# Paged decode attention inside a hybrid step: the five score stages of a half batch issued as one run in front of the value products

## The chip, the cores and the metric

The kernel runs on one core of one Trainium2 chip. The metric is the device time of one execution in microseconds (us). The kernel before took 1226.16 us (median of three executions, 1226.01 to 1227.58).

## The reference

One layer of a decoder serves 512 prompt tokens and 8 sequences of 4 new tokens each with shared weights. Cut to what the change touches, the latent attention of the new tokens over their paged past:

```python
past_c = cache_kv_latent[l][page_table].reshape(Bs, past_len, KV_LORA)   # 8 x 4096 x 256
past_r = cache_k_rope[l][page_table].reshape(Bs, past_len, QK_ROPE)      # 8 x 4096 x 64
s = (einsum('bqhr,bsr->bhqs', ql, c_kv) + einsum('bqhd,bsd->bhqs', qr, k_rope)) * scale
p = softmax(where(k_pos <= qp, s, -inf))
o = einsum('bhqs,bsr->bqhr', p, c_kv)
```

Around it stand two gated feed-forward blocks, a gated linear recurrence, the prompt's own attention and the projections, all in fp32.

## The kernel before

The large products take each fp32 operand as a high and a low part and sum three products (lines 225 to 262). While the decode attention runs (0.71 to 0.93 ms of the span) two generators are interleaved by the loop at line 1645: `decode()` (line 1557), and `phase_a()` (line 728), which finishes the second half of the output projection and runs the first 8 column tiles of the second feed-forward block for the prompt. The matmuls of `phase_a` are line 248: 128 rows by 128 columns of weights, 256 or, from 738 us on, 512 moving columns.

Decode works on 16 halves, two per sequence; a half is 2048 past keys in two blocks. For each half:

- `gather` (line 1477) and `gather_r` (line 1486): POOL issues indirect DMAs that bring the latent rows into one of seven slots (`ma`, `dx0`, `dx1`, `q0`, `ha`, `hb`, `mb`) and the rotary rows into `rraw`.
- `turn(st)` (line 1493): two 32x32 block transposes on VectorE (DVE, line 1498) write one stage of turned keys into a buffer `kh`. Stage 0 is the rotary part, stages 1 to 4 are 64 latent columns each. There are `KHB` = 4 buffers.
- `score(st)` (line 1501): eight products of 64 rows by 32 columns (line 1510; the profile counts each fp32 product as two matmuls, so 16), one in each of the eight 64x32 tiles of the array. After the last stage ScalarE (ACT) copies the odd column groups to `odd` (line 1518), and DVE adds them and takes the maximum (line 1519), called "top" below.
- `peak` (line 1521): a small matmul `pm` (line 1523) turns the maxima; DVE reduces (1525) and scales (1528); ACT takes the exponential (1529); DVE transposes to `pt` (1531); six ACT copies and two DVE copies spread it into `pbuf` (1537).
- `value(mate, c)` (line 1539): eight products of 128 rows by 32 columns for each block (line 1546; 16 matmuls in the profile).

Below, S run means score products of line 1510 that follow each other, V run the 32 value matmuls of a half, S(k) and V(k) those of half k (0 to 15), top(k) and pm(k) likewise.

The step loop at lines 1577 to 1605 places these. In iteration `n` it scores half n-2, takes the peak of half n-3 at step 1 and its values at step 4, and turns one stage per step. `RUNS` says that stages 0, 1, 2 are scored at step 2 and stages 3, 4 at step 4, in front of the values. The build then orders each engine's instructions by its own list scheduler, so a run as written can be cut where it places other ready work in between. A shared helper `tmp` (line 161) hands out scratch tiles by tag, two buffers each; `ssq` and `sq1` are also used by the sums of squares of lines 677, 717 and 267, which end before half 1 is scored.

Of the kernel before, what the change touches and what calls it, by code (L numbers as in the profile page):

```python
# [9 lines left out]
F32 = mybir.dt.float32  # L10
# [5 lines left out]
ALU = mybir.AluOpType  # L16
AX = mybir.AxisListType

P = 128
# [22 lines left out]
ROWS = 8  # L42
# [17 lines left out]
NW = 2  # L60
PRE, BODY = 22, 95
JS = ((8, 9), (0, 1), (2, 3), (4, 5), (6, 7))
KHB = 4
PEAK = 1
RUNS = {2: (0, 1, 2), 4: (3, 4)}
LEVELS = (32, 16, 8, 4, 2, 1)
CH = 64

# [39 lines left out]
def hybrid_step_kernel(  # L108
# [5 lines left out]
    nc = tc.nc  # L114
# [12 lines left out]
    def mk(shape, dt, tag, bufs=1, pool=None):  # L127
        return (pool or cur[-1]).tile(shape, dt, name=tag, tag=tag, bufs=bufs)
# [32 lines left out]
    def tmp(tag, n, bufs=2, pool=sb):  # L161
        return mk([P, HM], F32, tag, bufs, pool=pool)[:, :n]
# [70 lines left out]
    def gemm(wt, act_):  # L233
        wh, wl, kt = wt
        acc = ps("acc", "acc")
        n = act_[0].shape[-1]
        mm3(acc[:, :n], [((wh[:, k], wl[:, k]), (act_[0][:, k], act_[1][:, k])) for k in range(kt)])
        return acc[:, :n]
# [309 lines left out]
    with scope("ffn0") as pool:  # L548
# [4 lines left out]
        l, r = [u[:, lo4] for u in ux], [u[:, hi4] for u in ux]  # L553
# [56 lines left out]
        if True:  # L610
            if True:
                sst.close()
                st = stg.enter_context(tc.tile_pool(name="st", bufs=1, side="right", reuse_waits="tile"))
# [198 lines left out]
    with scope("mix") as mx_:  # L812
# [291 lines left out]
        with scope("at2"):  # L1104
# [6 lines left out]
            with scope("kv"):  # L1111
# [43 lines left out]
                for g in range(2):  # L1155
                    w = weight([w_qr[2 * g + i] for i in range(2)], KQ)
                    a = [gemm(w, Q[x]) for x in BOTH]
# [262 lines left out]
    with scope("dec"):  # L1420
# [48 lines left out]
        class Half:  # L1469
# [23 lines left out]
            def turn(self, st):  # L1493
                kh = mk([P, 2, ROWS, 2, 32], F32, "kh", KHB)
                j = JS[st][0]
# [5 lines left out]
            def score(self, st):  # L1501
                q = qbd[self.b % 2]
                if st == 0:
                    self.s = [ps("s", own=True) for _ in range(2)]
                for jj, j in enumerate(JS[st]):
                    for g in range(2):
                        c = (2 * jj + g) * 32
                        for r in range(2):
                            rs = slice(r * 64, r * 64 + 64)
                            nc.tensor.matmul(self.s[r][c : c + 32, : 2 * P], q[rs, j], self.kh[st][rs, g, :, jj], start=st == 0, stop=st == len(JS) - 1, skip_group_check=True)  # L1510
                if st == 1 and self.i and self.b + 1 < NB:
                    qsplit(self.b + 1)
                if st < len(JS) - 1:
                    return
                odd = mk([64, 2, 2 * P], F32, "odd")
                self.mx = mk([P, 1], F32, "mxh", 2)
                for r in range(2):
                    nc.scalar.copy(odd[:, r], self.s[r][64:, : 2 * P])
                    self.top = nc.vector.tensor_tensor_reduce(self.e[r * 64 : r * 64 + 64], self.s[r][:64, : 2 * P], odd[:, r], 1.0, -3.0e38, ALU.add, ALU.max, self.mx[r * 64 : r * 64 + 64])

            def peak(self):
                pm = ps("pm", "pm")[:, :P]
                nc.tensor.matmul(pm, self.mx.broadcast_to([P, P]), ident, start=True, stop=True, skip_group_check=True)
                m = m3[:, self.i, self.bs]
                nc.vector.tensor_reduce(m, pm.rearrange("p (g q) -> p q g", q=16), axis=AX.X, op=ALU.max)
                mq = mk([P, 16], F32, "mq", 2)
                mb = mk([P, 1], F32, "mbd", 2)
                nc.vector.scalar_tensor_tensor(mq, m, -SCALE, selL, op0=ALU.mult, op1=ALU.mult, accum_out=mb)
                nc.scalar.activation(self.e, self.e, AF.Exp, scale=SCALE, bias=mb, accum_out=Lc[:, self.i, 0, self.b : self.b + 1])
                pt = mk([P, ROWS, 32], F32, "pt", 2)  # L1530
                nc.vector.transpose(pt.rearrange("p a k -> p (a k)"), self.e)
                for r in range(2):
                    for g in range(2):
                        for h_ in range(2):
                            src = pt[(2 * r + g) * 32 : (2 * r + g) * 32 + 32, :, h_ * 16 : h_ * 16 + 16]
                            to = self.p[(2 * r + h_) * 32 : (2 * r + h_) * 32 + 32, g, :, self.i * 16 : self.i * 16 + 16]
                            (nc.scalar.copy if g + h_ else nc.vector.tensor_copy)(to, src)
# [19 lines left out]
        def decode():  # L1557
            H = [Half(n) for n in range(NH2)]
            blocks = [h_ for h_ in H for _ in range(2)]
            ups = [(h_, st) for h_ in H for st in range(len(JS))]  # L1560

            def gather(n=1):
                for h_ in blocks[:n]:
                    h_.gather()
                del blocks[:n]

            def turn(top):
                if ups:
                    h_, st = ups.pop(0)
                    if h_.n + st == 0:  # L1570
                        top = pin[0]
                    with tc.issue_after(top.ins) if top is not None else nullcontext():
                        h_.turn(st)
                    if st == 0 and h_.n + 1 < NH2:
                        H[h_.n + 1].gather_r()

            for n in range(NH2 + 4):

                def at(k):
                    return H[n - k] if 0 <= n - k < NH2 else None  # L1580

                for st in range(len(JS)):
                    if at(2):
                        for k in RUNS.get(st, ()):
                            at(2).score(k)
                    if n < 2 and st == 0:
                        if n == 0:
                            H[0].gather_r()
                        gather(2)
                        if n:  # L1590
                            nc.gpsimd.memset(pbuf, 0.0)
                    if n == 2 and st == 3:
                        gather(3)
                    if st == PEAK and at(3):
                        at(3).peak()
                    if st == 1 and at(4) and at(4).i:
                        at(4).gathered()
                    if st == len(JS) - 1 and at(3):
                        for c in range(2):
                            at(3).value(at(4), c)  # L1600
                            gather()
                    if n > 1 or n == 1 and st >= 1:
                        if n != 2 or st >= 2:
                            turn(at(2).top if at(2) and st == len(JS) - 1 else None)
                    yield

        def decode_end():
            uvf = mk([P, 2, NH, P], F32, "kh", KHB)
            for j in range(2):
# [130 lines left out]
    with scope("ffn1") as pool:  # L1740
# [96 lines left out]
        st = stg.enter_context(tc.tile_pool(name="st2", bufs=1, side="right", reuse_waits="tile"))  # L1837
# [113 lines left out]
```

## Time and profile before

| | before |
|---|---|
| median of three executions | 1226.16 us |
| the profiled execution | 1225.88 us |
| its span, first to last instruction | 1224.0 us |
| TensorE matmul (PE) busy | 1197.8 us, 98% |
| VectorE (DVE) busy | 986.6 us, 81% |
| ScalarE (ACT) busy | 693.6 us, 57% |
| line 1510, score matmuls | 1280, 47.2 us busy |

Busy time of an engine counts the time in which at least one of its instructions runs; matmuls overlap each other, so a matmul of 0.38 us does not cost 0.38 us. What a matmul costs is read from the distance between starts in the timeline. The profiled execution spent 1.9 us outside its span.

### The profile page before, as it was taken

Reading aid. Unit: us, or ns where it says so; the run is one execution under the profiler, and the core shown is the slowest. Engines: PE = TensorE matmul, PEld = TensorE weight load, DVE = VectorE, ACT = ScalarE, POOL = GpSimd, SP = SyncE. Lnnn points to the kernel's source line nnn. Section 1 sums busy time; section 2 is a strip of 40 time slices with the busy share of each in tenths; the row PEclk is TensorE's granted clock in tenths of the full one; section 3 lists DMA queues with packets and bytes.
Section 4 is the critical chain, followed back from the end, with each engine's and each line's share of the span. In section 5 each row is a group of like instructions: output and inputs, shape, how many; then the busy total and the mean of one; then the engine's idle time right before and its main releaser. Section 6 shows DMA issues by size and latency. Waiting matters only on the chain.

```text
span 1224.0 us, 26742 instructions
## 1 busy us (share of the span) xinstructions
PE 1197.8 (98%) x10924; PEld 1092.4 (89%) x10924; DVE 986.6 (81%) x2008; ACT 693.6 (57%) x1447; POOL 97.7 (8%) x112
## 2 busy tenths in 40 slices
PE   8999999999999999999999999999999999999997
PEld 7999999999999989998998876666667999999996
DVE  7997887878678788886877789888985789778665
ACT  7765554454476654554758765455444465554373
POOL 0000000000000000000000123332321111000000
PEclk9999999999999999999999999999999999999999
DMA  6233333323254313333242486679876858533451
GB/s 242 70 121 104 104 101 94 101 80 105 83 186 142 116 56 104 90 92 108 95 141 86 163 343 209 231 266 356 277 258 163 262 211 286 163 107 118 103 149 74
DMA packets 78427, 188.43 MB, mean 154 GB/s; under 512 B 14032, under 2 KB 35568, under 8 KB 73824
## 3 DMA queue, kind: packets, MB, share of 16 engines
q1 hardware_dynamic: 58128, 115.50, 28.8%
q0 software_dynamic: 15440, 65.67, 16.5%
q10 hardware_dynamic: 4736, 5.55, 1.3%
q8 instruction: 85, 1.39, 0.5%
q14 instruction: 38, 0.31, 0.1%
HBM read 170.53 MB, written 16.16 MB: 153 GB/s over the span
## 4 chain that ended last, share of the span: by engine, by line
PE 81%; issue 6%; DVE 5%; ACT 3%; DMA 3%; POOL 1%; DVEq 0%; SPq 0%; ACTq 0%; POOLq 0%
PE acc L248 18%; PE dn L230 12%; PE Y L449 11%; PE acc L230 8%; PE Z L449 7%; PE X L449 7%; PE acc L1853 3%; PE acc L628 3%; PE s L1510 3%; PE o L1546 2%; DVE kh L1498 1%; DMA ma<-w_g 1%; PE pa L976 1%; DMA mb<-w_u 1%; PE s L1226 1%
## 5 line engine op out<-in xcount | busy, mean ns | idle before, releaser
L248 PE MATMUL acc<-uh,wh 128*128 128x272 f32 (+2 forms) x496 | 160.9, 324 | 0.0
L248 PE MATMUL acc<-ul,wh 128*128 128x272 f32 (+2 forms) x496 | 156.3, 315 | 1.0 <-DVE ul L196 1.0
L248 PE MATMUL acc<-uh,wl 128*128 128x272 f32 (+2 forms) x496 | 155.7, 314 | 0.5 <-issue 0.5
L230 PE MATMUL dn<-hh,dh 128*128 128x272 f32 x384 | 111.3, 290 | 0.1
L230 PE MATMUL dn<-hh,dl 128*128 128x272 f32 x384 | 110.7, 288 | 0.0
L230 PE MATMUL dn<-hl,dh 128*128 128x272 f32 x384 | 110.5, 288 | 0.0
L222 DVE TENSOR_TENSOR wl<-wraw,wh 128x1024 fp32r<-128x1024 f32 (+2 forms) x78 | 83.6, 1074 | 31.7 <-ACT wh L221 31.1
L248 PEld LDWEIGHTS acc<-uh,wh 128*128 128x128 f32 x496 | 93.4, 188 | 17.1 <-issue 12.7
L221 ACT CAST wh<-wraw 128x1024 fp32r<-128x1024 f32 (+2 forms) x78 | 72.6, 932 | 57.8 <-PE acc L248 37.8
L248 PEld LDWEIGHTS acc<-ul,wh 128*128 128x128 f32 x496 | 93.5, 188 | 7.7 <-DVE ul L196 2.0
L248 PEld LDWEIGHTS acc<-uh,wl 128*128 128x128 f32 x496 | 93.3, 188 | 6.3 <-issue 1.5
L230 PEld LDWEIGHTS dn<-hh,dh 128*128 128x128 f32 x384 | 72.3, 188 | 1.0 <-DVE ha L498 0.3
L230 PEld LDWEIGHTS dn<-hl,dh 128*128 128x128 f32 x384 | 72.4, 188 | 0.0
L230 PEld LDWEIGHTS dn<-hh,dl 128*128 128x128 f32 x384 | 72.2, 188 | 0.0
L158 ACT CAST wh<-wraw 128x512 fp32r<-128x512 f32 (+1 forms) x68 | 41.2, 643 | 46.8 <-PE Z L449 33.1
L158 ACT CAST sh<-wraw 128x512 fp32r<-128x512 f32 (+1 forms) x67 | 40.9, 651 | 32.0 <-PE Z L449 20.1
L158 ACT CAST dh<-wraw 128x512 fp32r<-128x512 f32 x48 | 29.7, 620 | 48.1 <-PE dn L230 46.1
L159 DVE TENSOR_TENSOR wl<-wraw,wh 128x512 fp32r<-128x512 f32 (+1 forms) x68 | 46.5, 717 | 5.1 <-ACT wh L158 3.8
L159 DVE TENSOR_TENSOR sl<-wraw,sh 128x512 fp32r<-128x512 f32 (+1 forms) x67 | 46.9, 724 | 1.5 <-ACT sh L158 0.8
L1510 PE MATMUL s<-kh,q 64*32 64x256 f32 x1280 | 47.2, 382 | 0.0
L1490 POOL DMA_INDIRECT rraw<-pool_r,idx x32 | 32.9, 1027 | 142.0 <-DVE kh L1498 105.2
L501 ACT COPY tq<-X 128x272 f32<-128x272 f32 x31 | 11.9, 385 | 54.9 <-PE X L449 54.3
(723 smaller groups left out, 4122.0 us busy)
## 6 DMA issues: line engine op xcount, KB each, us to landing
wraw<-w_u SPq DMA_DIRECT2D x44, 512.0 KB
wraw<-w_g SPq DMA_DIRECT2D x43, 512.0 KB
wraw<-w_d SPq DMA_DIRECT2D x24, 512.0 KB
wraw<-w_in SPq DMA_DIRECT2D x24, 512.0 KB
wraw<-w_o SPq DMA_DIRECT2D x16, 512.0 KB
wraw<-w_d SPq DMA_DIRECT2D x16, 384.0 KB
wraw<-w_d SPq DMA_DIRECT2D x16, 256.0 KB
mA<-s_post ACTq DMA_DIRECT2D x16, 136.0 KB
```

Of the source, the lines that this page charges most:

```text
L158: nc.scalar.copy(hi, src)
L159: (eng or nc.vector).tensor_tensor(lo, src, f32(hi), op=ALU.subtract)
L221: nc.scalar.copy(wh[:, :kt], w[:, :kt])
L222: low[0] = nc.vector.tensor_tensor(wl[:, :kt], w[:, :kt], f32(wh[:, :kt]), op=ALU.subtract)
L230: mark[2] = nc.tensor.matmul(out, a, b, start=n == 0, stop=n == last).ins
L248: nc.tensor.matmul(acc[:, :n], a[:, k], b[:, k], start=k + i == 0, stop=k == kt - 1 and i == 2)
L449: mark[2] = nc.tensor.matmul(bank, a[p][:, k], b[q][:, k], start=first and k + n == 0, stop=k == 3 and n == 2, skip_group_check=True).ins
L628: nc.tensor.matmul(accs[x, d], wts[d][p][:, k], hs[k // 2][q][:, k % 2, x], start=k + n == 0, stop=k == nf - 1 and n == 2)
L1490: nc.gpsimd.indirect_dma_start(rraw.rearrange("p a r -> p (a r)"), None, pool_r, off)
L1510: nc.tensor.matmul(self.s[r][c : c + 32, : 2 * P], q[rs, j], self.kh[st][rs, g, :, jj], start=st == 0, stop=st == len(JS) - 1, skip_group_ ...
L1546: nc.tensor.matmul(o[g : g + 32, :R], self.p[:, c, a], self.craw[c][:, a], start=i + c == 0 and a < 4, stop=i + c == 2 and a >= 4, skip_gr ...
L1853: nc.tensor.matmul(accs[x, d], wts[d][p][:, k], hs[k // 2][q][:, k % 2, x], start=k + n == 0, stop=k == nf - 1 and n == 2)
```

## The change

`KHB` goes from 4 to 6, and `RUNS` gives way to `RUN` = 4: all five stages of a half are scored at step 4, in front of the values of the half before. To make room, `odd` becomes two separate tiles from the `ssq` scratch tag and `pt` a tile from the `sq1` tag; their own buffers go away. No arithmetic is added or removed.

```diff
-KHB = 4
+KHB = 6
...
-RUNS = {2: (0, 1, 2), 4: (3, 4)}
+RUN = 4
...
-                odd = mk([64, 2, 2 * P], F32, "odd")
                 self.mx = mk([P, 1], F32, "mxh", 2)
                 for r in range(2):
-                    nc.scalar.copy(odd[:, r], self.s[r][64:, : 2 * P])
-                    self.top = nc.vector.tensor_tensor_reduce(self.e[r * 64 : r * 64 + 64], self.s[r][:64, : 2 * P], odd[:, r], 1.0, -3.0e38, ALU.add, ALU.max, self.mx[r * 64 : r * 64 + 64])
+                    odd = tmp("ssq", 2 * P)[:64]
+                    nc.scalar.copy(odd, self.s[r][64:, : 2 * P])
+                    self.top = nc.vector.tensor_tensor_reduce(self.e[r * 64 : r * 64 + 64], self.s[r][:64, : 2 * P], odd, 1.0, -3.0e38, ALU.add, ALU.max, self.mx[r * 64 : r * 64 + 64])
...
-                pt = mk([P, ROWS, 32], F32, "pt", 2)
-                nc.vector.transpose(pt.rearrange("p a k -> p (a k)"), self.e)
+                pt = tmp("sq1", ROWS * 32)
+                nc.vector.transpose(pt, self.e)
+                pt = pt.rearrange("p (a k) -> p a k", k=32)
...
                     if at(2):
-                        for k in RUNS.get(st, ()):
+                        for k in range(len(JS)) if st == RUN else ():
                             at(2).score(k)
```

What the scheduler makes of it is seen in the order of the built programs. In these rows a count such as x24 is of products of the program (two matmuls each in the profile), and `q_8212` holds the queries.

PE around S(5), before:

```order
L1523 MATMUL pm<-ident,mxh 128x128
L1554 MATMUL o<-q_8212,q_8247 128x32 x2
L1510 MATMUL s<-kh,q_8212 32x256 x24
...
L1510 MATMUL s<-kh,q_8212 32x256 x16
L1546 MATMUL o<-dx_9532,pbuf 32x256 x8
```

PE around S(5), now:

```order
L1523 MATMUL pm<-ident,mxh 128x128
L1555 MATMUL o<-q_8212,q_8247 128x32 x2
...
L1510 MATMUL s<-kh,q_8212 32x256 x40
L1547 MATMUL o<-dx_9534,pbuf 32x256 x8
L1547 MATMUL o<-dx_9695,pbuf 32x256 x8
```

The left-out rows are 12 matmuls of line 248 on either side: they stood between the two S runs and stand in front of one now. The same happens in halves 6 and 11 to 15, and in 1 and 3.

PE around S(4), now:

```order
L1523 MATMUL pm<-ident,mxh 128x128
...
L1510 MATMUL s<-kh,q_8212 32x256 x18
...
L1510 MATMUL s<-kh,q_8212 32x256 x22
L1547 MATMUL o<-mb,pbuf 32x256 x8
L1547 MATMUL o<-ma,pbuf 32x256 x8
```

Here the scheduler put 10 matmuls of line 248 into the run, after the second product of stage 2; before, this half stood as x24 and x16. Half 7 is now 17 and 23, half 8 is 1 and 39, half 9 is 2 and 38, half 10 is 18 and 22. Half 0 stands in eight pieces (1, 8, 8, 1, 1, 2, 1, 18) in place of seven (24, 1, 4, 2, 1, 1, 7), half 2 in one in place of three (5, 19, 16). V(1) stands ahead of S(2) now, where it stood behind it.

DVE between half 0's `pbuf` copies and half 1's first turned maximum, one piece of the difference:

```order
 L1498 STREAM_TRANSPOSE kh<-rraw 128x512 x2
 L743 TENSOR_TENSOR sil<-acc,rn 128x512
-L1519 ISA q_8212,mxh<-s,odd 64x256
-L1519 ISA mxh 64x1
-L1519 ISA q_8212,mxh<-s,odd 64x256
+L222 TENSOR_TENSOR wl<-wraw,wh 128x1024 x2
+L1519 ISA q_8212,mxh<-s,ssq 64x256
+L1519 ISA mxh 64x1
+L1519 ISA q_8212,mxh<-s,ssq 64x256
 L1519 ISA mxh 64x1
```

Two splits of feed-forward weights (line 222) stand ahead of top(1) now; one of them stood behind it, the other further on.

DVE in half 13 from the reduction to `pt`, before and now:

```order
L1525 TENSOR_REDUCE q_8212<-pm 128x16
L222 TENSOR_TENSOR wl<-wraw,wh 128x1024
L745 TENSOR_TENSOR sil<-sil,sit 128x512
L1528 SCALAR_TENSOR_TENSOR mq,mbd<-q_8212 128x16
L1498 STREAM_TRANSPOSE kh<-ma 128x512
L1498 STREAM_TRANSPOSE kh<-dx_11211 128x512
L1531 STREAM_TRANSPOSE pt<-q_8212 128x256
```

```order
L1525 TENSOR_REDUCE q_8212<-pm 128x16
L1498 STREAM_TRANSPOSE kh<-ma 128x512
L1528 SCALAR_TENSOR_TENSOR mq,mbd<-q_8212 128x16
L745 TENSOR_TENSOR sil<-sil,sit 128x512
L1498 STREAM_TRANSPOSE kh<-dx_11224 128x512
L1531 STREAM_TRANSPOSE sq_11426<-q_8212 128x256
```

The weight split of line 222 has left this chain; it stands ahead of top(13) now.

## Rows read from the trace of the kernel before

**Rows 1.** The page: busy time by engine, and the chain's shares by engine.
```profile
PE 1197.8 (98%) x10924; PEld 1092.4 (89%) x10924; DVE 986.6 (81%) x2008; ACT 693.6 (57%) x1447; POOL 97.7 (8%) x112
PE 81%; issue 6%; DVE 5%; ACT 3%; DMA 3%; POOL 1%; DVEq 0%; SPq 0%; ACTq 0%; POOLq 0%
```
**Rows 2.** Busy time by stretch: length, then each engine (instructions); clock, DMA share, GB/s.
```profile
740.00:770.00 30.00, 28.09 (x319) 17.80 (x309) 28.19 (x70) 15.59 (x40) 8.15 (x8) 1.00 0.67 228
...
860.00:890.00 30.00, 29.87 (x360) 20.35 (x359) 28.65 (x66) 15.15 (x38) 9.48 (x10) 1.00 0.82 276
```
**Rows 3.** Timeline of PE, S(4) and V(3): start, length, instruction, [idle before, releaser].
```profile
780.58 0.40 PE L248 MATMUL acc<-uh,wl 128*128 128x512 f32 x1
780.91 1.53 PE L1510 MATMUL s<-kh,q 64*32 64x256 f32 x48
782.36 0.50 PE L248 MATMUL acc<-uh,wh 128*128 128x512 f32 x1
782.70 0.39 PE L248 MATMUL acc<-ul,wh 128*128 128x512 f32 x1
782.93 0.39 PE L248 MATMUL acc<-uh,wl 128*128 128x512 f32 x1
...
785.34 1.09 PE L1510 MATMUL s<-kh,q 64*32 64x256 f32 x32
786.36 1.07 PE L1546 MATMUL o<-mb,pbuf 128*32 128x256 f32 x16
787.25 1.05 PE L1546 MATMUL o<-ma,pbuf 128*32 128x256 f32 x16
```
**Rows 4.** Timeline of PE, two short pieces of S(0).
```profile
733.04 0.62 PE L1510 MATMUL s<-kh,q 64*32 64x256 f32 x2
734.01 0.66 PE L1510 MATMUL s<-kh,q 64*32 64x256 f32 x14
```
**Rows 5.** Timeline of PE, blocks of V(0), V(1), V(2), V(6) and V(13).
```profile
746.17 1.07 PE L1546 MATMUL o<-ma,pbuf 128*32 128x256 f32 x16 [0.48 <-ACT pbuf L1537]
...
761.78 1.81 PE L1546 MATMUL o<-q,pbuf 128*32 128x256 f32 x16
...
774.45 1.07 PE L1546 MATMUL o<-ha,pbuf 128*32 128x256 f32 x16
...
821.34 2.23 PE L1546 MATMUL o<-mb,pbuf 128*32 128x256 f32 x16
...
905.37 1.07 PE L1546 MATMUL o<-hb,pbuf 128*32 128x256 f32 x16 [0.85 <-ACT pbuf L1537]
```
**Rows 6.** Timeline of DVE around half 0's fifth stage, and a wait of PE.
```profile
725.13 0.66 DVE L1498 STREAM_TRANSPOSE kh<-dx 128x512 f32<-128x512 f32 x1
PE acc L248 <- DVE ul L196: 1.0, 1, 1.0
```
**Rows 7.** Timeline at half 1: PE's wait for top(1), and DVE's work around it.
```profile
748.54 0.71 PE L1451 MATMUL b<-ident,rs_t 128*128 128x128 f32 x4 [0.44 <-DVE mxh L1519]
748.06 0.42 DVE L1519 CUSTOM_DVE_ANT_0 q<-s,odd 64x256 f32<-64x256 f32 x1 [0.24 <-ACT odd L1518]
750.20 1.18 DVE L222 TENSOR_TENSOR wl<-wraw,wh 128x1024 fp32r<-128x1024 f32 x1
```
**Rows 8.** Timeline of DVE and ACT in half 2: end of top(2), pt, six pbuf copies.
```profile
763.82 0.07 DVE L1519 DVE_READ_ACCUMULATOR2_ANT mxh<- 64x1 f32 x1
...
768.13 0.41 DVE L1531 STREAM_TRANSPOSE pt<-q 128x256 f32<-128x256 f32 x1
768.58 1.84 ACT L1537 COPY pbuf<-pt 32x128 f32<-32x128 f32 x6 [0.53 <-DVE pt L1531]
```
**Rows 9.** Timeline of ACT and DVE in half 13: six pbuf copies, and the split of line 222.
```profile
904.10 1.84 ACT L1537 COPY pbuf<-pt 32x128 f32<-32x128 f32 x6 [0.94 <-DVE pt L1531]
900.62 1.21 DVE L222 TENSOR_TENSOR wl<-wraw,wh 128x1024 fp32r<-128x1024 f32 x1
```
**Rows 10.** DMA queues between 820 and 824 us: packets, MB, share.
```profile
q8 instruction: 1, 0.02, 1.4%
```

## The prediction

> **What bounds the kernel now.** I read the page first, then the busy time by stretch, then the timeline of PE through one half, then the waits. PE is busy 98% of the span and 81% of the chain that ended last is its work [rows 1], so a microsecond less of PE's time in the decode stretch is nearly a microsecond less of the whole, while work on ACT and POOL counts only where PE waits for it. DVE is close behind: between 740 and 770 us it is busy 28.19 of 30 us, as much as PE, and between 860 and 890 us 28.65 [rows 2]. So two questions decide: what the joined S runs save on PE, and whether what PE waits for still comes in time from DVE.
>
> **What an S run costs.** In the timeline of half 4 [rows 3] the step from one matmul of line 248 to the next is 0.23 us (782.70 to 782.93). From the one at 780.58 to the one at 782.70 it is 2.12 us, with three stages (x48) and one further matmul between. Two ordinary steps off, the run costs 2.12 - 2 x 0.23 = 1.66 us. Two stages last 1.09 us and three 1.53, so a stage costs 0.44. Three stages make 1.32, and 0.33 to 0.34 us are left that a run costs whatever its length; I take 0.33.
>
> The pieces of half 0 show a second thing [rows 4]: two score matmuls last 0.62 us and fourteen 0.66. Eight tiles work side by side, and a piece of a stage takes about as long as the stage. I take 0.44 us for a stage cut in two, once more than whole.
>
> **The merges.** Halves 5, 6 and 11 to 15 have one S run, joined to V, where they had two. Seven runs at 0.33: **-2.3 us**, if nothing is late for the run.
>
> **The cuts.** Halves 4, 7, 8, 9 and 10 still have two runs, since line 248 was placed inside: 18 and 22, 17 and 23, 1 and 39, 2 and 38, 18 and 22 products. Before, they were cut at 24, after the third whole stage (eight products each); now the cut falls inside a stage. No run is saved and a stage is paid twice: 5 x 0.44 = **+2.2 us**. Bounds: nothing, if the tiles still at work at the cut don't hold up the next matmuls, and 5 x 0.66 = 3.3, if a small piece costs its whole length [rows 4].
>
> The Trainium skill (TensorEngine Tiling (Array Packing), Tiling Modes, Key Properties) says that a change of the tiling mode drains TensorE and that tiles work independently. By that, only the number of changes counts, which gives the gain of the first rival below; rows 4 speak against it, since a piece with a seventh of the matmuls lasts nearly as long.
>
> **Half 0.** It stands in eight pieces for seven, and again inside stages: +0.33 + 0.44 = +0.8. Its two transposes of the fifth stage (0.66 each) moved ahead on DVE, out of the place where PE waited 1.0 for `ul` [rows 6]. Together -0.2; but V(0) began after 0.48 us of waiting for `pbuf` [rows 5], whose chain (top, `pm`, `pt`, copies) is not touched, so both, and half 1's merge, end in that wait: **0**, between -0.5 and +0.8.
>
> **Halves 1 to 3.** On DVE two splits of line 222 now stand ahead of top(1). One lasted 1.18 us, and DVE had 0.24 us idle before top(1) at 748.06 [rows 7]. So top(1) starts at about 748.06 - 0.24 + 2 x 1.18 = 750.2 and PE, whose matmul of line 1451 is next behind V(0) and waits for top(1), goes on at about 750.5 in place of 748.5: +2.0 us. Against this: half 2's S, in three pieces (5, 19, 16) with one cut inside a stage, is one run now (2 x 0.33 + 0.44 = -1.1); half 3 saves a run (-0.33); and V(1), with a second block of 1.81 us where an undisturbed one takes 1.05 to 1.07 [rows 3, 5], moves ahead of S(2). PE would so reach V(2) within 1 us of its old 774.45. There the other chain decides. S(2) now ends late, I estimate at 766.6: V(1) at 758.8 (31 matmuls of line 248 and a `pm` behind 750.5), its two blocks 1.9, nine matmuls 2.1, half 2's queries 1.3, five stages and the fixed part 2.5. Its top then ends near 768.0; it ended at 763.9 before, and from there to the end of `pt` took 4.6 us with six transposes between [rows 8]. Four of them with the other small steps and the split of 0.6 make some 5.1: `pt` at 773.1. The first block needs four of the six copies, 0.31 each: 774.3. V(2) starts at about 774.4 as before: **-0.1**, with ends -1.0 and +2.0 (the whole delay stays).
>
> **Half 13.** V(13) waited 0.85 us for `pbuf` [rows 5]. Its six copies came 0.94 us late, behind `pt`, and in front of `pt` stood a split of 1.21 us [rows 9], which has left this chain: **-0.85**. It goes ahead of top(13); there some 15 matmuls of line 248 cover it.
>
> **What costs nothing.** Six buffers for four let transposes run earlier; DVE's work is the same. `odd` and `pt` from shared scratch: the other users have ended before half 1 is scored, and two buffers each are what they had or more. The gathers keep their slots; a slot is freed at V, whose place among line 248's matmuls is the same from half 2 on. The cover is PE's other work, about 30 matmuls (7 us) in a half; without it, each `kh` that is late shows its transposes, 1.3 us a pair.
>
> **V runs that stop.** Some V blocks last longer and name no releaser: 1.81 us in V(1), 2.23 in V(6) [rows 5], 0.76 and 1.18 too much. About when the second stood still, a packet of PE's instructions came in [rows 10]. I carry these stops over as they are: 0. Both ways are rivals below.
>
> **Sum.** -2.3 + 2.2 + 0 - 0.1 - 0.85 = -1.05. The profiled execution took 1225.88, 0.28 under the median of the runs; 1224.8 against it, **1225.1 us** as a median.
>
> **Rivals.**
>
> *Faster: the stops go, or the cuts are free.* 40 products now stand ahead of the 32 of V. If PE stops because a V run begins before `pbuf` or the next instructions are there, 2.5 us of scores cover it. 0.48, 0.76 and 1.18 would go: 1225.1 - 2.4 = 1222.7. If mode changes alone count (39 tiled runs before, 30 now), 9 x 0.33 = -3.0 and -0.85 take the place of the sum: 1222.3. Both together give 1219.9. For it: no releaser is named, and most halves run clean [rows 3]. Against: rows 4, and that S(6) already stood in front of V(6). Chance 0.25.
>
> *Slower: instruction supply.* A run of S and V in one is now 80 + 64 profiled matmuls of a few hundredths of a microsecond each, with as many weight loads, 4.4 us without a long matmul between; before, at most 32 + 32 in 2.9. PE's instructions come in packets, and if they are spent faster than they land, each such run stops for about 1.2 us [rows 5, 10]. With three more stops the gain is gone; from there it decides. Five more: 1225.1 + 5 x 1.18 = 1231.0. For it: the stops are already in V runs. Against: half 4's run took no stop [rows 3].
>
> The Trainium skill (Runtime: NRT & Kernel Launch, Instruction fetch mechanics) says that the next block of instructions is fetched while the current one runs, and that crossing a block is mostly hidden. By that this rival is worth nothing; rows 10 show the packet beside a stopped run, so that the trace does not bear it out in that place. Chance 0.18.
>
> *No change: DVE becomes the bound.* At 28.65 of 30 us [rows 2] it can't go much faster; what PE saves would return as waits for `kh` of the last stages or for `pbuf`. The merges and half 13 (3.15) come back, the cuts stay half hidden: about 1226. Chance 0.10.
>
> **How the numbers follow.** My own case has 0.47, with a range of its own of 1222.5 to 1227.0 (cuts free to 3.3, halves 1 to 3 from -1.0 to +2.0, not all at once). 0.2% is 2.45 us, about what a measurement of this kernel can tell from no change: faster is below 1223.7, slower above 1228.6. Faster holds the first rival (0.25) and the low end of my case: 0.35. Slower holds most of the second rival and the high end of halves 1 to 3: 0.18. The rest is 0.47. The range for 8 in 10 goes from 1220.5 (nearly both parts of the first rival) to 1229.5 (three to four more stops).
>
> **What would show it.** Right: score runs of x80 of 2.2 to 2.6 us, a fixed part of 0.33 saved in each of seven halves; in the five cut halves pieces that each last whole stages; PE's line 1451 waiting about 2 us near 750; V(2) near 774.4; no wait for `pbuf` in V(13). Wrong: waits of PE for `kh` inside runs, V blocks of 2 us in more halves than now, or in none, and short pieces after which line 248 goes on at once.

## The result

The changed kernel took 1234.8 us (median of six executions, 1232.9 to 1236.35), the kernel before 1227.15 us (six, 1226.01 to 1228.39): a ratio of 1.0064, 95% interval 1.0054 to 1.0074. It is slower by 7.7 us. The forecast was 1225.1 us, with a range of 1220.5 to 1229.5.

The profiled execution took 1232.9 us, with a span of 1231.1. The page of the changed kernel, busy time and chain, against [rows 1]:

```profile
PE 1201.1 (98%) x10924; PEld 1096.8 (89%) x10924; DVE 985.9 (80%) x2008; ACT 694.4 (56%) x1447; POOL 98.8 (8%) x112
...
PE 87%; DVE 7%; ACT 3%; DMA 2%; issue 1%; DVEq 0%; SPq 0%; ACTq 0%
```

Every engine on the page has as many instructions as before, and PE is the chain even more (87% against 81%). Busy time does not tell what happened: on PE it rose by 3.3 us with the same 10924 matmuls. Two other views tell it.

**First, the waits.** PE's waits between 740 and 935 us, by what ended them (the releaser), in us, times, longest:

```profile
PE acc L248 <- DVE wl L222: 4.5, 4, 1.8
PE b L1451 <- DVE mxh L1519: 1.9, 1, 1.9
PE o L1547 <- ACT pbuf L1538: 0.7, 2, 0.4
```

The second line is the wait that was forecast at 2.0 us, [rows 7] before with 0.44. The first one is new: the matmuls of line 248 waited four times for the low part of their weights. The largest is in half 4, where the scheduler had put ten of them into the S run. Timeline of PE there:

```profile
782.04 1.49 PE L1510 MATMUL s<-kh,q 64*32 64x256 f32 x36
785.31 0.50 PE L248 MATMUL acc<-uh,wl 128*128 128x512 f32 x1 [1.78 <-DVE wl L222]
...
787.82 1.51 PE L1510 MATMUL s<-kh,q 64*32 64x256 f32 x44
```

And of DVE, from the end of top(3) to the split that PE waited for:

```profile
777.36 0.08 DVE L1519 DVE_READ_ACCUMULATOR2_ANT mxh<- 64x1 f32 x1
777.47 1.90 DVE L1498 STREAM_TRANSPOSE kh<-dx 128x512 f32<-128x512 f32 x3
779.29 0.65 DVE L745 TENSOR_TENSOR sil<-sil,sit 128x512 f32<-128x512 f32 x1
779.86 1.89 DVE L1498 STREAM_TRANSPOSE kh<-dx 128x512 f32<-128x512 f32 x3
...
781.85 0.69 DVE L1498 STREAM_TRANSPOSE kh<-dx 128x512 f32<-128x512 f32 x1
...
784.07 1.18 DVE L222 TENSOR_TENSOR wl<-wraw,wh 128x1024 fp32r<-128x1024 f32 x1
```

Eight transposes of turned keys (one more stands at 782.52) are between the top and the split. The input of this split, a cast on ACT, had ended at 770.11 us; DVE came to it 14.0 us later and was not idle in between. The matmul that waits for it is the one at 782.93 in [rows 3], which did not wait: in the kernel before DVE did this split 0.5 us after its cast, and it ended 6 us ahead of S(4):

```profile
773.42 1.20 DVE L222 TENSOR_TENSOR wl<-wraw,wh 128x1024 fp32r<-128x1024 f32 x1
```

**Second, the runs themselves.** Two joined runs of the changed kernel in the timeline of PE, S(13) with V(12) and S(14) with V(13):

```profile
900.36 3.80 PE L1510 MATMUL s<-kh,q 64*32 64x256 f32 x80
...
911.94 2.39 PE L1510 MATMUL s<-kh,q 64*32 64x256 f32 x80
```

The same 80 matmuls, 3.80 us and 2.39. The granted clock does not part them, nor does the load on the DMA engines, as a stretch of this S(13) and one of S(15), which is as clean as S(14), show (last three columns: clock, DMA share, GB/s):

```profile
901.50:903.60 2.10, 1.89 (x43) 0.96 (x36) 0.17 (x1) 0.00 (x0) 1.00 (x1) 1.00 0.78 200
924.00:926.00 2.00, 2.00 (x81) 1.43 (x80) 1.59 (x4) 1.91 (x6) 0.00 (x0) 1.00 0.90 268
```

What DVE and POOL did at the first:

```profile
900.48 1.18 DVE L222 TENSOR_TENSOR wl<-wraw,wh 128x1024 fp32r<-128x1024 f32 x1
904.64 0.42 DVE L1519 CUSTOM_DVE_ANT_0 q<-s,ssq 64x256 f32<-64x256 f32 x1 [2.97 <-ACT ssq L1518]
```

```profile
900.24 0.95 POOL L1490 DMA_INDIRECT rraw<-pool_r,idx  x1 [5.99 <-DVE kh L1498]
901.49 1.00 POOL L1490 DMA_INDIRECT rraw<-pool_r,idx  x1 [0.30 <-issue]
```

DVE had nothing left to do for 2.97 us, so the scores did not wait for keys. POOL issued the two rotary gathers for half 15, which it could do since DVE had just turned the rows of half 14. From S(14) on there are no more such gathers. I call it a stop where a run of this kind takes longer than an undisturbed one (2.89 us from S to the next line 248 for x32 with V, 4.18 for x80 with V; pieces of a cut half against the same piece in run e2 below) and no releaser is named. By that measure the kernel before had 3.9 us of stops: 0.9 in V(1), 1.2 each in V(6) and V(7) [rows 5], 0.1 and 0.3 in V(8) and V(12), and 0.2 in the first run of S(12), against 1.46 us for an undisturbed x48. (Another 0.3 in S(5) stands in run e3 below too, which has no such gathers.) The changed kernel has 8.2: 0.7, 1.9, 0.7, 1.1, 0.2 in the runs that end with V(3) to V(7), then 0.2, 2.0 and 1.4 with V(10) to V(12).

Where the time went, half by half (end of each V in the timelines, later or earlier than in the comparison kernel; left the two kernels of this case, right the same two orders without rotary gathers, runs e2 and e3 below):

| at the end of | scores in it | changed - before | step | e2 - e3 | step |
|---|---|---|---|---|---|
| V(2) | S(3) joined | +0.7 | | +0.4 | |
| V(3) | S(4) cut | +3.6 | +3.0 | +2.6 | +2.2 |
| V(4) | S(5) joined | +4.9 | +1.3 | +2.1 | -0.5 |
| V(5) | S(6) joined | +5.2 | +0.3 | +1.7 | -0.3 |
| V(6) | S(7) cut | +6.1 | +0.8 | +2.8 | +1.0 |
| V(7) | S(8) cut | +5.5 | -0.6 | +3.1 | +0.4 |
| V(8) | S(9) cut | +6.6 | +1.1 | +4.3 | +1.2 |
| V(9) | S(10) cut | +8.5 | +1.9 | +6.2 | +1.9 |
| V(14) | S(11) to S(15) joined | +8.5 | 0.0 | +4.4 | -1.9 |

V(k) means the end of that run. Without stops the staircase is plain: every joined run gains 0.3 to 0.5 us, every cut half loses 0.4 to 2.2. In the left columns the stops lie over it. Behind decode 1.4 us came back in the profiled pair, which the pair without gathers doesn't show; why stays open.

### The profile page after: what moved, and what is told of

Read it like the earlier page. It is cut to its first block, busy times and chain, and to the rows that moved or that the text cites. A ratio compares the mean times of both kernels' runs of the same rounds, so it can differ in the third digit from the quotient of the medians.

```text
span 1231.1 us, 26725 instructions
## 1 busy us (share of the span) xinstructions
PE 1201.1 (98%) x10924; PEld 1096.8 (89%) x10924; DVE 985.9 (80%) x2008; ACT 694.4 (56%) x1447; POOL 98.8 (8%) x112
## 4 chain that ended last, share of the span: by engine, by line
PE 87%; DVE 7%; ACT 3%; DMA 2%; issue 1%; DVEq 0%; SPq 0%; ACTq 0%
PE acc L248 20%; PE dn L230 11%; PE Y L449 11%; PE acc L230 10%; PE Z L449 7%; PE X L449 7%; PE acc L1854 3%; PE acc L628 3%; PE s L1510 3%; DVE kh L1498 2%; PE o L1547 2%; PE sr L1328 1%; PE pa L976 1%; DVE wl L222 1%; PE s L1226 1%
## 5 line engine op out<-in xcount | busy, mean ns | idle before, releaser
L1510 PE MATMUL s<-kh,q 64*32 64x256 f32 x1280 | 52.2, 381 | 1.4 <-issue 0.3
L1510 PEld LDWEIGHTS s<-kh,q 64*32 64x32 f32 x1280 | 26.1, 106 | 22.1 <-issue 9.4
```

## The experiments

The kernel before took 1226.2 to 1227.2 us on every chip used but one; on that one, where e1 to e4 ran, it took 1222.13, and no run there shows a stop. So ratios are compared, each to the kernel before on the same chip, and the two kinds of chip are told apart.

### Is it the order of the scores, the gathers, or the cuts?

**e1**, the old order on the new buffers:

```diff
-                        for k in range(len(JS)) if st == RUN else ():
+                        for k in RUNS.get(st, ()):
```

> The changed kernel's six buffers and shared scratch, with the score stages placed as before (three at step 2, two at step 4). If the loss lies in the order of the scores, this one is not slower than the kernel before: 1227 us, or some 2 to 3 us less, since half 0 and half 2 stand in two whole pieces here where they stood in seven and three. If the shared scratch or the transposes that run further ahead cost anything, it lies above 1229 us.

Measured: 0.9998 (0.9987 to 1.0009). This is no slower than the kernel before, so the loss came with the order of the scores. But the trace shows that two effects cancel here. Against e3, on the same chip, the whole halves 0 and 1 gained 2.7 us up to V(0), and halves 7, 9 and 10 lost 0.6, 1.1 and 1.5. There PE waits for late splits in the old order too; the waits, and the one in half 10:

```profile
PE acc L248 <- DVE wl L222: 2.3, 3, 1.2
...
853.49 0.50 PE L248 MATMUL acc<-uh,wl 128*128 128x512 f32 x1 [1.23 <-DVE wl L222]
```

The same three matmuls wait in halves 7, 9 and 10 of the changed kernel, for 2.7 of its 4.5 us. So three of the four late splits come with the buffers in either order, and only half 4's, 1.8 us, with the joined run. From the cast of a weight to its split took 1.3 us in the kernel before, 2.9 here and 3.7 in the changed kernel (mean of the 18 splits from about 760 to 900 us): with six buffers transposes stand ahead of the split. Whether five or six buffers or the shared scratch bring this was not tried one by one.

**e2** and **e3**, the changed kernel and the kernel before with one pair of rotary gathers for all halves:

```diff
-                        H[h_.n + 1].gather_r()
+                        H[h_.n + 1].rraw = H[0].rraw
```

> The changed kernel with the rotary rows gathered once, for half 0, and used by all halves; 30 of the 32 rotary gathers are left out, the order on PE is the same. Theory 1: PE stops inside a joined run where a rotary gather is issued and lands during it. Then the stops in halves 4 to 7, 12 and 13 (0.5 + 1.8 + 0.7 + 1.0 + 2.0 + 1.4 = 7.4 us in the profile of the changed kernel) go, and the time is about 1227.5 us. Theory 2: a joined run stops because its 224 instructions are issued faster than they are supplied, whatever else happens. Then the stops stay and the time is 1233 to 1236 us.

> The kernel before with the rotary rows gathered once, for half 0. Theory 1: the stops in V(1), V(4), V(6), V(7) and V(12) (0.9 + 0.3 + 1.2 + 1.2 + 0.3 = 3.9 us) go: about 1223 us. Theory 2: they stay, 1226 to 1228 us.

Measured: 1.0043 (1.0030 to 1.0055) and 0.9996 (0.9986 to 1.0006). On a chip without stops these could not decide about stops; what they give is the right half of the table, the cost of the order and the buffers without stops: +5 us, with the same four waits for `wl`, 4.5 us. Against e1, which has the same buffers and ran on the same chip, the cut halves 7 to 10 lose only 0.4, 0.4, 0.1 and 0.4 us in e2, and half 4 loses 2.2.

**e4**, the scores behind all matmuls of line 248 that were written before them, the values behind the scores:

```diff
-                            at(2).score(k)
+                            with tc.issue_after(pin[1]) if pin[1] is not None else nullcontext():
+                                at(2).score(k)
...
-                            at(3).value(at(4), c)
+                            with tc.issue_after(pin[2]) if 3 <= at(3).n < NH2 - 1 else nullcontext():
+                                at(3).value(at(4), c)
```

> The changed kernel with the scores of a half issued behind every matmul of line 248 written before them, and the values behind the scores, so that from half 3 on S and V stand in one whole run. The five cuts (some 0.6 us each in the changed kernel) go: -3 us. If the waits for the low part of the weights (4.5 us in four of the cut halves) come from the cut, where the matmuls of line 248 stand too early, they are to a part covered elsewhere: 1227 to 1230 us. If they come from VectorE being late in any order, they stand ahead of the run now and the time is about 1232 us. The stops of theories 1 and 2 are not touched.

Measured: 1.0042 (1.0022 to 1.0063), no better than e2 on the same chip, though every run from half 4 on is whole and takes 4.18 us (`pin[1]` is the last matmul of line 248 written so far, `pin[2]` the last score). PE's waits:

```profile
PE acc L248 <- DVE wl L222: 4.6, 4, 2.0
PE acc L248 <- ACT wh L221: 2.4, 3, 1.2
```

The wait stands ahead of the run now. So the cuts are not the main cost: a wait that the scheduler foresees is there with or without them. The split is late either way.

**e0**, the changed kernel once more:

> The changed kernel itself, on the chip of these runs. In the four runs before this one no tiled run stopped without a named releaser, with rotary gathers or without, so the stops of the first two profiles may belong to the chip. If so, the profile shows none here, the waits for the low part of the weights (4.5 us) and the five cuts (3 us) are all that is left, and the ratio to the kernel before is about 1.004 (as without rotary gathers), in place of 1.0064. If the stops belong to the joined runs with their gathers, they are here too and the ratio is 1.006 or more.

Measured: 1.0067 (1.0052 to 1.0083) on a chip with stops; they stand in the same halves as in the first profile and are nearly as long (the run of S(13) took 5.59 us there, 5.53 here). They are no accident of one execution.

### Why the split is late

**e7**, the split of the low part ahead of older work on DVE while decode runs:

```diff
-        low[0] = nc.vector.tensor_tensor(wl[:, :kt], w[:, :kt], f32(wh[:, :kt]), op=ALU.subtract)
+        with tc.high_priority(EARLY) if ahead[0] else nullcontext():
+            low[0] = nc.vector.tensor_tensor(wl[:, :kt], w[:, :kt], f32(wh[:, :kt]), op=ALU.subtract)
```

with `EARLY` = 100, and **e9**, the same edit in the kernel before.

> The changed kernel with the split of the low part of the weights (line 222) put ahead of the transposes on VectorE while decode runs. Theory 3: a joined run frees five buffers of turned keys at once, their transposes come in one burst on VectorE ahead of the split, and PE waits for the split; the cuts are the same wait as the scheduler foresaw it. Then the waits (4.5 us) and the cuts (3 us) go together, every run from half 4 on is whole and gains 0.35 us on the kernel before, and the time is 7 to 8 us under the changed kernel's, a ratio of 0.997 to 0.999 to the kernel before. Rival: VectorE has no room in these halves, and what the split gains the keys lose. Then PE waits for turned keys or for pbuf instead, and the ratio stays at 1.003 or more.

> The kernel before with the same edit of line 222 alone. Theory 3: its transposes come stage by stage, the split was never late, so the ratio is 0.999 to 1.001. If it gains as much as the changed kernel does by the edit, the late split is not the joined runs' doing.

Measured: e7 1.0053 (1.0037 to 1.0068), e9 1.0004 (0.9994 to 1.0014). In e7 all cuts from half 4 on vanish by themselves, and the wait for `wl` falls to the last of these three lines:

```profile
PE o L1550 <- ACT pbuf L1541: 2.8, 3, 1.4
PE s L1513 <- DVE kh L1501: 1.8, 3, 1.0
...
PE acc L251 <- DVE wl L225: 0.7, 1, 0.7
```

So that part of theory 3 holds: splits behind transposes make both the waits and the cuts. The forecast of the time failed, and the rival's came true: the waits for `pbuf` and keys, 0.7 and 0.3 us in the changed kernel, grew by 3.6 us, and more whole runs caught more stops: the runs of S(8) and S(9), cut before, stop for 1.6 and 2.2 us. In the kernel before the split is hardly late, and the edit does nothing.

**e10**, as e7, with halves 0 to 3 in the old order, run on two chips:

```diff
-                        for k in range(len(JS)) if st == RUN else ():
+                        for k in RUNS.get(st, ()) if at(2).n < 4 else range(len(JS)) if st == RUN else ():
```

> As the run with the split first, but halves 0 to 3 scored in the old order (three stages at step 2, two at step 4), so that only halves 4 to 15 have a joined run. By theory 3 halves 0 to 3 no longer lose what they lost (some 3 us at S(3), 2 us at top(1)), the twelve joined halves gain 0.35 us each (4.2 us), and the ratio to the kernel before is 0.995 to 0.997. If the joined runs lose elsewhere what they save, it is 0.999 to 1.001.

> The kernel with joined runs from half 4 on once more, as the measure for the two beside it. The stops without a named releaser were there on the chip of the last four runs, 12.7 us of them in this kernel, and not on the chip of the four before. With them its ratio to the kernel before is 1.001 to 1.003, without them 0.995 to 0.998.

Measured: 1.0022 (1.0012 to 1.0032) and 1.0027 (1.0017 to 1.0036). Twelve whole runs, no wait for `wl` over 0.7 us, and still slower than before: nine of the twelve runs take 4.3 to 6.5 us in place of 4.18.

### What a stop is

**e12**, e10 without the rotary gathers, beside e10b on the same chip; the edit is that of e2.

> The same kernel with the rotary rows gathered once, for half 0, and used by all halves (30 of 32 rotary gathers left out). Theory 1: the stops come from a rotary gather that is issued and lands while a long run is on PE. On a chip that has them (see the run beside it) they go here, and the ratio to the kernel before is 0.988 to 0.992. Theory 2: a long run outruns the supply of PE's instructions by itself. Then they stay, and the ratio is that of the run beside it. On a chip without stops the two kernels are the same to 0.1%.

Measured: 0.9899 (0.9883 to 0.9916), 15 us under its neighbour. The runs of S(12) and S(13), first in e10b, timeline of PE and then of POOL:

```profile
881.78 2.26 PE L1514 MATMUL s<-kh,q 64*32 64x256 f32 x53
884.34 1.84 PE L1514 MATMUL s<-kh,q 64*32 64x256 f32 x27 [0.31 <-issue]
...
895.80 4.42 PE L1514 MATMUL s<-kh,q 64*32 64x256 f32 x80
```

```profile
882.25 0.95 POOL L1494 DMA_INDIRECT rraw<-pool_r,idx  x1 [4.72 <-DVE kh L1502]
883.51 0.95 POOL L1494 DMA_INDIRECT rraw<-pool_r,idx  x1 [0.31 <-issue]
...
896.80 0.94 POOL L1494 DMA_INDIRECT rraw<-pool_r,idx  x1 [7.12 <-DVE kh L1502]
898.05 0.95 POOL L1494 DMA_INDIRECT rraw<-pool_r,idx  x1 [0.30 <-issue]
```

and the first of them in e12 (the second takes 2.39 us too):

```profile
871.36 2.39 PE L1514 MATMUL s<-kh,q 64*32 64x256 f32 x80
```

With the gathers gone the long runs are clean: eleven of the twelve are within 0.1 us of 4.18, and the twelfth, S(14) with V(13), is 0.5 longer, with a wait for `pbuf` in it. The length of a run alone stops nothing: theory 2 falls, and with it the reason that the prediction gave for its slower rival.

The stops also keep time with the gathers. PE's weight loads (PEld) in S(12) of e10b, where they start again after each gap:

```profile
883.60 0.17 PEld L1514 LDWEIGHTS s<-kh,q 64*32 64x32 f32 x3 [0.39 <-issue]
884.35 0.16 PEld L1514 LDWEIGHTS s<-kh,q 64*32 64x32 f32 x4 [0.58 <-issue]
885.08 0.62 PEld L1514 LDWEIGHTS s<-kh,q 64*32 64x32 f32 x22 [0.57 <-issue]
```

That is 0.1, 0.8 and 1.6 us behind the start of the second gather, at 883.51. In the changed kernel eleven steps between two matmuls of these runs are 0.43 us or more and name no releaser; ten of them end within 0.1 us of one of these three distances.

**e18**, e10 with a plain load of the same size into the same buffer, issued by SyncE:

```diff
-                    off = bass.IndirectOffsetOnAxis(ap=idx[:, blk : blk + 1], axis=0)
-                    nc.gpsimd.indirect_dma_start(rraw.rearrange("p a r -> p (a r)"), None, pool_r, off)
+                    nc.sync.dma_start(rraw.rearrange("p a r -> p (a r)"), pool_r[blk * P : blk * P + P])
```

> The kernel with joined runs from half 4 on, with each rotary gather replaced by a plain load of 128 rows of the same pool, of the same size into the same buffer, issued by SyncE and not by POOL; the rows are not those of the page table. If the rows landing stop PE, the stops stay (12 us on a chip that has them, ratio 1.002). If POOL's issue of an indirect transfer does, they go: 0.989 to 0.992. A load that stands behind others in SyncE's queue may come late and make PE wait for keys; then the trace names them.

Measured: 0.9919 (0.9902 to 0.9937). S(12) on PE, and the two loads on SP's queue, issued as it begins:

```profile
870.79 2.39 PE L1513 MATMUL s<-kh,q 64*32 64x256 f32 x80
```

```profile
870.92 1.25 SPq L1493 DMA_DIRECT2D rraw<-pool_r  x2
```

As many bytes come at the same place, and PE does not stop, though the two complete kernels on this chip, e17 and e19 below, show stops. So it is not the landing of 512 KB in `rraw` as such, but the indirect transfer that POOL issues. Which part of that (the issue, the scattered rows, or how its pieces move) these runs don't part.

### The two together, and where the gathers may stand

**e16**, the changed kernel with both edits, split first and no rotary gathers:

> The changed kernel with the weight split first and the rotary rows gathered once, for half 0: both suspected causes are taken away, and halves 0 to 3 stay as the change has them. If late splits (with the cuts they make) and stops during rotary gathers are the whole loss, what is left are twelve runs that gain 0.35 us each, against some 3 us lost at S(3) and nothing at V(0) to V(1): on a chip with stops a ratio of 0.992 to 0.996, on a chip without them 0.996 to 1.000. If a third cause is left, it is over 1.000.

Measured: 0.9944 (0.9926 to 0.9962). With both causes away the joined order is faster than before, so no third cause of the size of the loss is left. Of the 7.6 us, about 3.9 are the stops of the kernel before, which keeps its gathers; that leaves some 3.7 for the order, an estimate.

Three complete kernels, all from e10, move the gathers. **e14**: four buffers for rotary rows and five for keys. **e17**: five key buffers alone. **e19**: each pair of rotary gathers behind the next two latent ones.

```diff
-                    rraw = mk([P, ROWS, RD], F32, "rraw", 2)
+                    rraw = mk([P, ROWS, RD], F32, "rraw", 4)
...
-KHB = 6
+KHB = 5
```

(e14 has both parts, e17 the second alone.) And e19:

```diff
-                        H[h_.n + 1].gather_r()
+                        later.append(H[h_.n + 1])
...
+                    if later and (st == len(JS) - 1 or not at(3)):
+                        with tc.issue_after(pin[1]) if at(3) and at(3).n > 3 else nullcontext():
+                            later.pop().gather_r()
```

> The same kernel, complete, with four buffers for the rotary rows in place of two and five for the turned keys in place of six. A rotary gather no longer waits for VectorE to turn the rows of the half before, which happens just ahead of a run; POOL issues it right behind the latent gathers, as V ends. Theory 1: it is then out of the next run's way, the stops go as without the gathers, and the ratio is 0.988 to 0.993 on a chip that has stops. Theory 2: they stay. Rival: it falls into the next run still, or five buffers of turned keys are too few and PE waits for keys; then 1.000 or more.

> The kernel with joined runs from half 4 on and the split first, with five buffers of turned keys in place of six, nothing else changed. If five buffers move the rotary transposes, and so the gathers, into the joined run's second half, as the trace of the run with four rotary buffers suggests, most stops go and the ratio is 0.993 to 0.997. If the four rotary buffers were what counted, it stays at 1.001 to 1.004.

> The kernel with joined runs from half 4 on, six key buffers, complete, with each pair of rotary gathers issued on POOL behind the two latent gathers that follow V in place of ahead of them. The latent gathers wait for V, so no rotary gather is issued while the run is on PE. Theory 1: the stops go, ratio 0.989 to 0.993 on a chip that has them, 0.995 to 0.998 on one that has not. Rival: the rotary rows come too late, their transposes fall into the time before the next run, and PE waits for keys: 1.000 or more.

Measured: e14 0.9944 (0.9927 to 0.9960), e17 0.9979 (0.9970 to 0.9989), e19 0.9983 (0.9971 to 0.9995). All three beat the kernel before and the changed one; e14 is the best, 1220.24 us against 1226.15. The reason that I gave for e14 was wrong. Its gathers are not issued as V ends; they still wait for keys to be turned, but that happens later, and they fall into the run's end. S(4) on PE, and the first of the two on POOL:

```profile
782.14 2.39 PE L1514 MATMUL s<-kh,q 64*32 64x256 f32 x80
```

```profile
784.65 0.95 POOL L1494 DMA_INDIRECT rraw<-pool_r,idx  x1 [8.18 <-DVE kh L1502]
```

With five key buffers the rotary transposes come later, here at 783.67 us, inside the run, where e10b issued the gathers at 783.03, ahead of its S(4). e17 shows that this is much of the gain; the rest of e14's is the four buffers or other waits, which is open. e19 does what e14 was meant to do. S(5) on PE and POOL behind it:

```profile
793.75 2.39 PE L1514 MATMUL s<-kh,q 64*32 64x256 f32 x80
```

```profile
797.44 0.94 POOL L1487 DMA_INDIRECT dx<-pool_c,idx  x1 [8.32 <-PE o L1551]
...
799.93 0.95 POOL L1494 DMA_INDIRECT rraw<-pool_r,idx  x1 [0.30 <-issue]
```

From S(5) on none of its runs stops for more than 0.1 us without a named releaser (`pin[1]` is the last latent gather here), but the rows then come late for the transposes in places (DVE is idle for 2.88 us until they land at 820.57), as its rival says. The waits for keys that the rival names did not grow (1.0 us, as in e12); PE waits 2.8 us for `pbuf` and 2.0 for `wl`.

**e15**, the old order with e14's buffers:

> The old order of the scores with the same buffers (four for rotary rows, five for turned keys, shared scratch). Theory 1: the 4.4 us of stops that the kernel before has on a chip that shows them go: ratio 0.995 to 0.998. Theory 2: 0.999 to 1.001. On a chip without stops both say 0.999 to 1.001.

Measured: 1.0013 (1.0003 to 1.0022), a miss. Stops of 0.4 to 1.1 us stay in V(3) to V(7), since the gathers follow the key transposes here too (V(1) is 1.1 us longer as well, but at a granted clock of 0.62, so this is no stop). And PE waits 4.6 us for `wl` in the old order, as in e1; with four key buffers it is 0.5 us at most (e3).

## Why the prediction was wrong

It forecast -1.05 us on the profiled execution, and +7.0 was measured. Step by step:

- **The cost of a run and the merges** held. An undisturbed joined run with V takes 4.385 us of PE's time, counted as in the prediction, against 1.655 + 3.086 in two parts, so the saving is 0.36 (forecast 0.33). Seven of them gain 2.8 us in the pair without gathers (forecast 2.3).
- **The cuts** were sized at 5 x 0.44 = 2.2 us, bounds 0 and 3.3. The five halves cost 6.8 (right columns of the table). The working held for the cut as such: against e1 the cuts of halves 7 to 10 cost 0.1 to 0.4 us each. The piece of two lasts 0.62 us as in rows 4, which gave the price:

```profile
834.65 0.62 PE L1510 MATMUL s<-kh,q 64*32 64x256 f32 x2
```

  The Trainium skill (TensorEngine Tiling (Array Packing), Tiling Modes, Key Properties) says that a change of the tiling mode drains TensorE. It gives no price; by that rule alone S(8), in two runs before and after, would have lost nothing, and it lost 0.4.

- **What failed** is the step before it: I took the cuts as the scheduler's free choice and did not ask why it cut, and I put "what costs nothing" at 0. In half 4 ten matmuls stood inside the run because their weights' low part was not there earlier. "DVE's work is the same" is true of the sum (985.9 us busy, 986.6 before) and false of the order: what stands behind the earlier transposes is not `kh`, which I priced, but `wl`, which I did not. PE waited 4.5 us for it. In half 4 (1.8 us) one long run had freed five key buffers at once, and eight transposes came ahead of the split; in halves 7, 9 and 10 (2.7 us) the buffers alone do it, as e1 shows.
- **Halves 0 to 3** held. Half 0 came out at -0.5 us, the low end of its range. The changed kernel was 0.7 us later already before half 0, where this execution had a granted clock of 0.50, TensorE's lower level of 1.2 GHz, from 699 to 702 us (PE had been busy 16.7 of the 19 us ahead of it), and the one before 1.00; less that, the wait for top(1), V(1), S(2) and V(2) came within 0.4 us of where the working had put them: 1.9 us for 2.0, then V(1) at 758.4 (758.8), S(2) ending by 766.7 (766.6), and V(2) at 774.4 (774.4):

```profile
759.14 1.07 PE L1547 MATMUL o<-dx,pbuf 128*32 128x256 f32 x16 [0.29 <-ACT pbuf L1538]
...
764.49 2.95 PE L1510 MATMUL s<-kh,q 64*32 64x256 f32 x80
...
771.00 3.17 PE L1510 MATMUL s<-kh,q 64*32 64x256 f32 x68
774.46 0.65 PE L1510 MATMUL s<-kh,q 64*32 64x256 f32 x12 [0.30 <-DVE kh L1498]
775.12 1.07 PE L1547 MATMUL o<-ha,pbuf 128*32 128x256 f32 x16
```

  S(3) waits inside the run for its last keys, so that x80 spreads over 4.1 us. The prediction had not seen this; a wait for `kh` inside a run was one of its signs of being wrong. It cost nothing, because `pbuf` came no earlier: the first block of V(2) needs four of these six copies, which end by 775.1 (estimate from this row):

```profile
773.85 1.84 ACT L1538 COPY pbuf<-sq 32x128 f32<-32x128 f32 x6 [0.94 <-DVE sq L1531]
```

- **Half 13**: the wait of V(13) for `pbuf` went, as forecast (-0.85). The run before it then stopped for 1.4 us.
- **"V runs that stop: I carry these over as they are: 0"** is the second step that failed. Stops went from 3.9 to 8.2 us, as a joined run is longer and stands where the gathers are issued. The slower rival had this sign and place, with 5 x 1.18 = 5.9 us, and it measured 4.3. Its mechanism was wrong: no supply that runs short by length, but POOL's gathers (e12, e18). Its count was wrong too, without effect on the sum: a V run has 32 matmuls in the profile, so that a joined run is 80 + 32 and not 80 + 64. The row on the instruction packet [rows 10] was a coincidence. Between 900 and 904.5 us, where S(13) stops, the DMA view lists two queues, none of them with instructions:

```profile
q0 software_dynamic: 134, 0.48, 41.3%
q1 hardware_dynamic: 132, 0.24, 15.3%
```

  And in the kernel before a packet came between 809 and 811 us, beside V(5), whose two blocks ran clean:

```profile
q8 instruction: 1, 0.02, 3.0%
```

  The rule of the Trainium skill (Runtime: NRT & Kernel Launch, Instruction fetch mechanics) that crossing a block of instructions is mostly hidden agrees with these two places.

- **The other rivals.** "Faster" would have been right without either cause (e16). "DVE becomes the bound" was near the truth, at a wrong place: DVE is not full, it is idle 20% of the span and 16% of the stretch from 740 to 930 us; its queue is in the wrong order at four moments.

The sum from the runs: merges -2.8, cuts with their waits +6.8 (3.2 in halves 7, 9 and 10 that e1 has as well, 2.2 in half 4, 1.3 for the other cuts), stops +4.3, half 13 -0.9, halves 0 to 3 with the 0.7 from before them +0.7. That makes +8.1 at V(14), where the table has +8.5; 1.4 came back behind decode.

## What to carry to other kernels

Before a long run of one kind on the busiest engine is called cheaper, look at what its length does to the others: it can free their buffers in one burst, which then stands in their queue ahead of small work with a nearer due time. More buffers for a producer can do the same without any long run (e1). When a scheduler cuts a run, ask what it was waiting for; here the late split cost more than the cut, and holding the run together moved the wait without shortening it. Stops without a named releaser deserve a table of what every other engine issued at that time, before they are carried over as a constant. A run that measures the same as its neighbour (e1) may hold two effects that cancel; compare where its halves end.

## What the runs showed of the hardware

- On three chips of four (the number is known for all runs but the first pair), indirect gathers issued by POOL while PE runs a long series of 64x32 and 128x32 matmuls held PE up for 0.2 to 2.3 us a run, in gaps that end some 0.1, 0.8 and 1.6 us behind the start of the second gather of a pair. Plain loads of the same size from SyncE do not (e18). The Trainium skill (DMA: Bandwidth & Descriptors, SWDGE vs HWDGE vs iDMA) says that descriptors of transfers from GpSimd are computed in software by a GpSimd core, and those of transfers from SyncE in hardware. That is a difference between the two kinds of transfer tried here; whether it is the one that counts for PE no run here shows.
- The stops repeat in the same halves in another execution (e0), and were absent on one chip, where the kernel before is 4 us faster than elsewhere, about the size of its stops (3.9).
- A gather behind the run (e19) costs PE nothing that the trace shows: it falls among the long matmuls of line 248. How long a series must be to be held up was not tried by itself.
